# Rotary tables spread by twelve transfers, later rounding of the index sums, slot order, and one moved gate product in a hybrid decoder layer

## The chip, the cores and the metric

The kernel runs on one core of a Trainium2 chip. The metric is the device time of one execution in microseconds (us), as the median of several runs. A profile of one more execution gives the times of single instructions.

## What is computed

One decoder layer on 512 tokens of width 1024, in float32:

```python
proj = x @ w_in
rq, rk, rv, rg, aq, ak, av, iq, ik, iw = jnp.split(proj, IN_SPLITS, axis=-1)
rq, rk, aq, ak, iq, ik = (rope(t, positions) for t in ...)
ret = group_norm(retention_chunkwise(rq, rk, rv)) * gain
ret = jax.nn.silu(rg) * ret
# index: logits[q, h, s] = relu(iq[q, h] . ik[s]); score = sum_h iw[q, h] * logits
sel = indexer_topk(iq, ik, iw, 128)           # 8 index heads of width 64, causal
att = sparse_attention(aq, ak, av, sel)       # softmax over the selected keys
x = layer_norm(ALPHA * x + concat([ret, att]) @ w_out)
gate, up = jnp.split(x @ w_gate_up, 2, axis=-1)
x = layer_norm(ALPHA * x + (silu(gate) * up) @ w_down)
```

## The kernel before

Every large product is made of three matmuls (`mm3`, lines 93 to 96): both operands are split into a rounded part in the format fp32r (names ending in h) and a rest (names ending in l). The split of a weight (`split`, lines 84 to 91) costs a cast on ACT (L86, tile `wh`) and either a subtraction on DVE (L91, tile `wl`) or, for the weights marked Q, a negated copy on ACT (L88) to which a DMA that POOL issues (L89) adds the raw weight.

The order of each engine's instructions is the order in which the program writes them. It has these stages:

1. The index projection (`acc0`, L205), 120 matmuls. Beside it `rotary_tables` works out the angles on DVE and their sines and cosines on ACT. DMAs then copy these from the compact tiles, which hold 256 positions in each half of the partitions, into the tile `tables`: `CT` and `ST` for heads of width 128 (8 transfers on SP's queue, L80), `CI` and `SI` for index heads of width 64 (16 transfers on POOL's queue, L167 and L168).
2. The feature projections (`proj_feature`, tile `pf`): 16 units of 24 matmuls with weights from the ring `wh`/`wl` of 4 buffers. Each unit's result is rotated by `rope` (L217 to L219 on DVE, the sum L221 on POOL) when the next unit has begun.
3. The token projections (`proj_token`, tile `pt`), with retention beside them.
4. The output projection (`mx`) with the attention, then the gate and up products (`g_cycle`, seven products A to D for each of 22 blocks, accumulated in `ga`, `gb`, `gc`), then the down projection.

Beside stages 2 and 3 runs a side chain: `index_rope` (rotation of the index key and queries, their split into h and l parts, and the DMAs that place the halves), `logits` (for each of 8 heads two matmuls on PE, a relu on ACT and one multiply-add on DVE, L375 and L377, on tile `score`), and `topk` (16 pairs of L388 and L389 for each block of 128 queries). `pace` hands out the side chain: in each slot of the main stage it gains a credit and runs the next piece while the credit is positive. `run` calls the side chains of one slot in the order in which they are given.

The psum pool has 4 buffers of the kind `u`, which the logits, the turns of retention (`ret_turn`, tile `rz`, read by `put_mix`, L436 and L437) and the attention scores (`as`, L538) share: a matmul into the fifth buffer waits until the first has been read.

## Time and profile before

| what | value |
|---|---|
| median of 3 runs | 639.75 us (638.44 to 640.84) |
| the profiled execution, its own time | 640.71 us |
| its span from first to last instruction | 638.3 us |
| PE busy | 622.2 us, 97% of the span |
| DVE busy | 486.2 us, 76% |
| ACT busy | 288.4 us, 45% |
| POOL busy | 109.6 us, 17% |
| granted clock of PE, mean | 0.996 |

PE takes the matmuls, PEld loads their weights beside it, DVE, ACT and POOL are the elementwise engines, SP only issues DMAs. Matmuls overlap, so an engine that shows as busy all the time can still have small gaps from one start to the next; times between two starts are given where that matters.

### The profile page before, as it was taken

To read this page: it belongs to the slowest core of one execution; us is meant where nothing else is said; L and a number is where in the kernel's file an instruction comes from. 1 tells how busy PE (TensorE), PEld (TensorE's weight loads), DVE (VectorE), ACT (ScalarE), POOL (GpSimd) and SP (SyncE) were. 2 spreads that over 40 slices of the span, in tenths; PEclk is the share of its full clock that TensorE was granted. 3 is DMA by queue.
4 is the path that set the end of the run, shared out by engine and by line. 5 is a ranking of instruction groups with operands and counts; after the bars stand their busy time and mean duration, and the time that the engine had idled before them with its cause. 6 is when DMAs were issued, how large, how long until landed. Compare 5 with 4: busy or idle time off the path is not lost.

```text
span 638.3 us, 9756 instructions
## 1 busy us (share of the span) xinstructions
PE 622.2 (97%) x3792; PEld 553.8 (87%) x3792; DVE 486.2 (76%) x893; ACT 288.4 (45%) x506; POOL 109.6 (17%) x117
## 2 busy tenths in 40 slices
PE   9999899999999999999999999999999999999995
PEld 7987688888887878888999999999999988888884
DVE  5758886988879877999988989889898874333256
ACT  5603544433343667445655555555455653311100
POOL 1559723321464000141000000000000000000011
PEclk9999999999999999999999999999999999999998
DMA  8865664679544862271823132231323352312002
GB/s 286 295 190 131 157 165 120 160 190 222 133 100 108 315 250 88 74 189 22 227 84 132 67 132 89 110 132 67 132 74 126 132 202 95 132 68 97 1 33 99
DMA packets 23855, 86.66 MB, mean 136 GB/s; under 512 B 2883, under 2 KB 3907, under 8 KB 18179
## 3 DMA queue, kind: packets, MB, share of 16 engines
q1 hardware_dynamic: 18448, 71.32, 32.3%
q0 software_dynamic: 4784, 13.64, 11.0%
q10 hardware_dynamic: 576, 1.11, 0.5%
q8 instruction: 29, 0.48, 0.3%
q14 instruction: 18, 0.12, 0.1%
HBM read 69.80 MB, written 2.10 MB: 113 GB/s over the span
## 4 chain that ended last, share of the span: by engine, by line
PE 54%; DVE 4%; issue 0%; POOLq 0%; ACT 0%; DVEq 0%
PE ga L787 20%; PE gc L787 10%; PE gb L787 5%; PE dl L94 3%; PE dl L96 3%; PE dl L95 3%; PE dr L96 3%; PE dr L94 3%; PE dr L95 3%; DVE wl L91 1%; DVE part L642 0%; PE mx L95 0%; DVE gs L762 0%; PE mx L96 0%; DVE x L615 0%
## 5 line engine op out<-in xcount | busy, mean ns | idle before, releaser
L426 POOL TENSOR_TENSOR rs<-ve,half 128x1 f32<-128x1 f32 (+1 forms) x11 | 13.6, 1238 | 383.7 <-DVE ve L425 383.6
L91 DVE TENSOR_TENSOR dl<-draw,dh 128x1024 fp32r<-128x1024 f32 x22 | 26.9, 1224 | 59.0 <-ACT dh L86 59.0
L86 ACT CAST wh<-raw 128x1024 fp32r<-128x1024 f32 x44 | 46.0, 1049 | 44.6 <-issue 16.7
L86 ACT CAST dh<-draw 128x1024 fp32r<-128x1024 f32 x22 | 23.1, 1052 | 68.0 <-PE dl L96 37.1
L96 PE MATMUL pf<-xh,wl 128*128 128x512 f32 x128 | 50.1, 391 | 2.2 <-DMA wl<-raw 2.2
L94 PE MATMUL pf<-xh,wh 128*128 128x512 f32 x128 | 50.0, 391 | 0.0
L95 PE MATMUL pf<-xl,wh 128*128 128x512 f32 x128 | 49.9, 390 | 0.0
L91 DVE TENSOR_TENSOR wl<-raw,wh 128x1024 fp32r<-128x1024 f32 x25 | 32.4, 1307 | 11.7 <-ACT wh L86 11.7
L94 PE MATMUL pt<-wh,xh 128*128 128x512 f32 x96 | 39.1, 407 | 0.0
L96 PE MATMUL pt<-wh,xl 128*128 128x512 f32 x96 | 37.5, 391 | 0.0
L95 PE MATMUL pt<-wl,xh 128*128 128x512 f32 x96 | 37.4, 390 | 0.0
L94 PE MATMUL dl<-dh,h 128*128 128x512 f32 x88 | 34.2, 389 | 0.0
L95 PE MATMUL dl<-dl,h 128*128 128x512 f32 x88 | 34.2, 389 | 0.0
L96 PE MATMUL dl<-dh,h 128*128 128x512 f32 x88 | 34.2, 389 | 0.0
L95 PE MATMUL dr<-dl,h 128*128 128x512 f32 (+1 forms) x88 | 33.4, 379 | 0.0
L96 PE MATMUL dr<-dh,h 128*128 128x512 f32 (+1 forms) x88 | 33.4, 379 | 0.0
L94 PE MATMUL dr<-dh,h 128*128 128x512 f32 (+1 forms) x88 | 33.4, 379 | 0.0
L96 PEld LDWEIGHTS pf<-xh,wl 128*128 128x128 f32 x128 | 24.0, 188 | 8.1 <-DMA wl<-raw 3.0
L762 DVE TENSOR_TENSOR gs<-graw,gs 128x512 f32<-128x512 f32 x44 | 30.3, 688 | 0.8
L762 DVE TENSOR_TENSOR gs<-graw 128x512 f32<-128x512 f32 x44 | 30.1, 684 | 0.0
L95 PEld LDWEIGHTS pf<-xl,wh 128*128 128x128 f32 x128 | 24.0, 188 | 4.7
L94 PEld LDWEIGHTS pf<-xh,wh 128*128 128x128 f32 x128 | 24.0, 188 | 4.6
(961 smaller groups left out, 1925.3 us busy)
## 6 DMA issues: line engine op xcount, KB each, us to landing
graw<-in_wgu_dram SPq DMA_DIRECT2D x22, 1024.0 KB, 4.8
draw<-in_wd_dram SPq DMA_DIRECT2D x22, 512.0 KB, 4.6
wl<-raw POOLq DMA_DIRECT2D x19, 512.0 KB, 5.8
raw<-in_wf_dram SPq DMA_DIRECT2D x8, 1024.0 KB, 7.5
raw<-in_wo_dram SPq DMA_DIRECT2D x8, 1024.0 KB, 5.7
raw<-in_wt_dram SPq DMA_DIRECT2D x6, 1024.0 KB, 5.0
w0s<-in_w_dram SPq DMA_DIRECT2D x8, 320.0 KB, 5.0
x<-in_x_dram SPq DMA_DIRECT2D x4, 512.0 KB, 5.0
```

The source lines that it names most:

```text
L86: A.copy(hi, src)
L91: eng_lo.tensor_tensor(lo, src, hi.bitcast(F32), op=ALU.subtract)
L94: T.matmul(acc, lhsT=lh, rhs=rh, start=first, stop=False, **kw)
L95: T.matmul(acc, lhsT=lh, rhs=rl, start=False, stop=False, **kw)
L96: T.matmul(acc, lhsT=ll, rhs=rh, start=False, stop=last, **kw)
L426: G.tensor_tensor(r[:, :n], e[:, :n], half[:, :n], op=ALU.pow)
L762: eng.tensor_tensor(t[dst], a, b, op=ALU.subtract)
L787: T.matmul(gp[n][acc], lhsT=a[:, i * S + k * P:i * S + k * P + P], rhs=parts[q][:, b, k], start=first and j == 0, stop=j == 11, skip_group ...
```

## The change

The change has four parts.

- **Tables.** The sines and cosines are written as two tiles `trig`, each with the cosine beside the sine (the second tile with the negated sine), so that one transfer carries both. 8 transfers of 32 partitions fill `CI` and `SI`, 3 of them issued by POOL, 3 by SP and 2 by ACT; 4 transfers of 64 partitions on SP then fill `CT` and `ST`. The cosine is computed twice, and the absolute value comes first on ACT.
- **Index sums.** DVE writes the unrounded sums (`ks`, `qs`); POOL no longer adds them a second time. The rounding (`kh`, `qa`, `qb`) is done by copies on ACT, and all of it stands one step of the side chain later. The first step yields 1.7 instead of 2.7, the last one is followed by one more rounding, and the side chain starts with a credit of 0 instead of -1.
- **Slot order.** Beside `proj_token(0)` the retention and attention chain `tail` now comes ahead of the side chain in each slot.
- **Gate product.** The product D of gate block 1 is taken out of cycle 1 and put into cycle 2, between the two products C, with its weights in a tile of its own (`s9`); the end of block 1 (`g_end`) moves with it.

```diff
--- before.py
+++ after.py
@@ -122,8 +122,9 @@
     CT, ST, CI, SI = (tables[:, i] for i in range(4))
 
     def rotary_tables():
-        both = [tmp("angles"), tmp("turns"), tmp("trig"), tmp("trig_n")]
-        (ang, rr), (hh, kk), (cs, sn), (ng, _) = ((t[:, :H], t[:, H:]) for t in both)
+        both = [tmp("angles"), tmp("turns")]
+        (ang, rr), (hh, kk) = ((t[:, :H], t[:, H:]) for t in both)
+        trig = [tmp(f"trig{q}").rearrange("p (k c) -> p k c", k=2) for q in range(2)]
 
         def sub_mul(dst, mult, const_, src):
             V.scalar_tensor_tensor(dst, in0=mult, scalar=-const_, in1=src, op0=ALU.mult, op1=ALU.add)
@@ -152,20 +153,19 @@
         nearest(kk, ang, 1.0 / TWO_PI)
         sub_mul(ang, kk, TWO_PI, ang)
         yield
-        A.activation(sn, ang, AF.Sin)
         A.activation(rr, ang, AF.Abs)
-        A.activation(cs, rr, AF.Sin, scale=-1.0, bias=cols[:, 2:3])
-        A.activation(ng, ang, AF.Sin, scale=-1.0)
+        for q in range(2):
+            A.activation(trig[q][:, 0], rr, AF.Sin, scale=-1.0, bias=cols[:, 2:3])
+            A.activation(trig[q][:, 1], ang, AF.Sin, scale=(1.0, -1.0)[q])
+        queues = (nc.gpsimd, nc.sync, nc.scalar)
+        for i in range(2):
+            ps, at = slice(64 * i, 64 * i + 64, 2), slice(H * i, H * i + H)
+            for q in range(4):
+                queues[(4 * i + q) % 3].dma_start(tables[32 * q:32 * q + 32, 2:, at], trig[q // 2][ps])
         for i in range(2):
             ps, at = slice(64 * i, 64 * i + 64), slice(H * i, H * i + H)
             for q in range(2):
-                dma(CT[64 * q:64 * q + 64, at], cs[ps])
-                dma(ST[64 * q:64 * q + 64, at], (sn, ng)[q][ps])
-        for i in range(2):
-            ps, at = slice(64 * i, 64 * i + 64, 2), slice(H * i, H * i + H)
-            for q in range(4):
-                nc.gpsimd.dma_start(CI[32 * q:32 * q + 32, at], cs[ps])
-                nc.gpsimd.dma_start(SI[32 * q:32 * q + 32, at], (sn, ng)[q // 2][ps])
+                dma(tables[64 * q:64 * q + 64, :2, at], trig[q][ps])
         yield
 
 
@@ -234,28 +234,37 @@
         G.memset(kk3[:, 1:].bitcast(F32), 0.0)
         A.activation(iwr, acc0[0], AF.Copy, scale=IDX_SCALE)
         t1, t2 = rope(None, acc0[0], CI, SI)
-        V.tensor_tensor(kh, t1, t2, op=ALU.add)
         ks = tmp("ks")
-        G.tensor_tensor(ks, t1, t2, op=ALU.add)
-        for b in (0, 64):
-            s, d = slice(b, b + 32), slice(b + 32, b + 64)
-            G.tensor_tensor(kl[0][s], ks[s], kh[s].bitcast(F32), op=ALU.subtract)
-            nc.gpsimd.dma_start(kl[1][d].bitcast(F32), kl[0][s].bitcast(F32))
-            nc.gpsimd.dma_start(kh[d].bitcast(F32), kh[s].bitcast(F32))
-        yield 2.7
-        for i in range(4):
-            t1, t2 = rope(None, acc0[1 + i], CI, SI, P)
-            V.tensor_tensor(qa[:, i], t1[:, P:], t2[:, P:], op=ALU.add)
-            qs = tmp("qs")
-            G.tensor_tensor(qs[:, P:], t1[:, P:], t2[:, P:], op=ALU.add)
+        V.tensor_tensor(ks, t1, t2, op=ALU.add)
+        yield 1.7
+
+        def halves_k():
+            A.copy(kh, ks)
+            for b in (0, 64):
+                s, d = slice(b, b + 32), slice(b + 32, b + 64)
+                G.tensor_tensor(kl[0][s], ks[s], kh[s].bitcast(F32), op=ALU.subtract)
+                nc.gpsimd.dma_start(kl[1][d].bitcast(F32), kl[0][s].bitcast(F32))
+                nc.gpsimd.dma_start(kh[d].bitcast(F32), kh[s].bitcast(F32))
+
+        def halves_q(i, qs):
+            A.copy(qa[:, i], qs[:, P:])
+            A.copy(qb[:, i], qs[:, P:])
             G.tensor_tensor(ql[:, i], qs[:, P:], qa[:, i].bitcast(F32), op=ALU.subtract)
-            A.copy(qb[:, i], qa[:, i].bitcast(F32))
             if i % 2:
                 n = slice(i - 1, i + 1)
                 for d, s in ((qa[32:64, n], ql[0:32, n]), (qa[96:128, n], ql[64:96, n]),
                              (qb[0:32, n], ql[32:64, n]), (qb[64:96, n], ql[96:128, n])):
                     nc.gpsimd.dma_start(d.bitcast(F32), s.bitcast(F32))
+
+        rounding = halves_k
+        for i in range(4):
+            t1, t2 = rope(None, acc0[1 + i], CI, SI, P)
+            qs = tmp("qs")
+            V.tensor_tensor(qs[:, P:], t1[:, P:], t2[:, P:], op=ALU.add)
+            rounding()
+            rounding = lambda i=i, qs=qs: halves_q(i, qs)
             yield 2.3
+        rounding()
         yield 3.0
         iwp = psu("iwp")
         for j in range(1, NB):
@@ -579,7 +588,7 @@
     lg = chain(*[logits(j) for j in range(1, NB)])
     tk = chain(*[topk(j) for j in range(1, NB)])
     side = chain(index_rope(), lg, tk)
-    run(chain(*[proj_feature(c) for c in range(4)]), pace(side, 0.85, -1.0))
+    run(chain(*[proj_feature(c) for c in range(4)]), pace(side, 0.85))
     run(chain(*[proj_feature(c) for c in range(4, 8)]), pace(side, 0.85))
     run(proj_token(1), pace(side, 1.7))
     rt["decay"] = big.tile([P, 2, HEADS * P], F32, tag="s7", name="decay")
@@ -588,7 +597,7 @@
     rets = retention()
     run(proj_token(2), pace(side, 1.8), pace(rets, 1.2))
     tail = chain(rets, att_score(0))
-    run(proj_token(0), pace(side, 0.9), pace(tail, 1.4))
+    run(proj_token(0), pace(tail, 1.4), pace(side, 0.9))
     drain(tail)
 
 
@@ -761,13 +770,19 @@
         for dst, a, b in ((0, u[:, :S], g[:, :S]), (1, u[:, S:], t[0]), (2, u[:, S:], u[:, :S]), (3, g[:, S:], t[1]))[which]:
             eng.tensor_tensor(t[dst], a, b, op=ALU.subtract)
 
+    def held(n):
+        return n == FIRST - 3
+
     def g_conv(n, kind, eng=V, into=None):
         if n >= NF:
             return
         g, u, t = graw[n][:, 0], graw[n][:, 1], gsum.get(n)
         src = {"A": lambda: (t[1], t[0]), "B": lambda: (g[:, :S], g[:, S:]), "C": lambda: (t[2], t[3]),
                "D": lambda: (u[:, S:],)}[kind]()
-        if into:
+        if kind == "D" and held(n):
+            both = big.tile([P, 2, S], F32R, tag="s9", name="dheld")
+            h, l = both[:, 0], both[:, 1]
+        elif into:
             hl = big.tile([P, 2, 1024], F32R, tag=into, name=f"g{n}{kind}")
             h, l = hl[:, 0], hl[:, 1]
         else:
@@ -815,7 +830,7 @@
     def g_cycle(n, between=None):
         nxt = n + 1 if FIRST <= n + 1 < NF else None
         g_mm(n, "a", "A", 0, "s2", False)
-        if n:
+        if n and not held(n - 1):
             g_end(n - 1)
         if between:
             next(between)
@@ -835,6 +850,8 @@
         if nxt:
             g_t1(nxt)
             g_mm(nxt, "b", "B", 1, "12", True)
+        if held(n - 1):
+            g_mm(n - 1, "c", "D", 0, "s4", False)
         c = gp[n]["c"]
         if n == NF - 1:
             c = tmp("gc")[:, :Q]
@@ -844,6 +861,8 @@
         V.tensor_tensor(gp[n]["t7"], gp[n]["t7"], c, op=ALU.add)
         if between:
             next(between)
+        if held(n - 1):
+            g_end(n - 1)
         if n == 0:
             g_conv(1, "A")
         if n + 2 >= FIRST:
@@ -857,7 +876,7 @@
         if n == 0:
             for m in range(FIRST):
                 g_silu1(m)
-        if n < NF - 1:
+        if n < NF - 1 and not held(n):
             g_mm(n, "c", "D", 0, "s4", False)
         A.activation(gp[n]["h2"], gp[n]["a"], AF.Silu)
         g_conv(n + 1, "D", V if n else None)
```

On ACT, at the end of stage 1, before (`trig` and `trig_n` are the compact sines and cosines, `wh_372` and `wh_376` the first two feature weights):

```order
L86 CAST w0h_307<-w0s_83 128x640
L155 ACT_TABLE_LOAD
L155 ACTIVATE trig<-angles 128x256
L156 ACTIVATE angles<-angles 128x256
L157 ACTIVATE trig<-angles,cols 128x256
L158 ACTIVATE trig_n<-angles 128x256
L86 CAST wh_372<-raw_275 128x1024
L86 CAST wh_376<-raw_275 128x1024
```

and after the change:

```order
L86 CAST w0h_307<-w0s_83 128x640
L156 ACTIVATE angles<-angles 128x256
L158 ACT_TABLE_LOAD
L158 ACTIVATE trig_175<-angles,cols 128x256
L159 ACTIVATE trig_175<-angles 128x256
L158 ACTIVATE trig_176<-angles,cols 128x256
L159 ACTIVATE trig_176<-angles 128x256
L164 DMA tables<-trig_176 32x2x256
L164 DMA tables<-trig_175 32x2x256
L86 CAST wh_361<-raw_275 128x1024
L86 CAST wh_365<-raw_275 128x1024
```

The load of the sine table now stands behind the absolute value, and a fifth activation and two DMA issues stand ahead of the first feature weight.

On POOL, in the index part of stage 2, before (`ks`, `qs` are the second sums, `wl_483` the second weight that POOL finishes):

```order
L239 TENSOR_TENSOR ks<-rt_415,rt_416 128x512
L242 TENSOR_TENSOR kk_359<-ks,kk_359 32x512
L243 DMA kk_359<-kk_359 32x512
L244 DMA kk_359<-kk_359 32x512
L242 TENSOR_TENSOR kk_359<-ks,kk_359 32x512
L243 DMA kk_359<-kk_359 32x512
L244 DMA kk_359<-kk_359 32x512
L221 TENSOR_TENSOR akT<-rt_445,rt_446 128x512
L250 TENSOR_TENSOR qs<-rt_466,rt_467 128x384
L251 TENSOR_TENSOR ql<-qs,qa 128x384
L89 DMA wl_483<-raw_279 128x1024
```

and after the change:

```order
L245 TENSOR_TENSOR kk_348<-ks,kk_348 32x512
L246 DMA kk_348<-kk_348 32x512
L247 DMA kk_348<-kk_348 32x512
L245 TENSOR_TENSOR kk_348<-ks,kk_348 32x512
L246 DMA kk_348<-kk_348 32x512
L247 DMA kk_348<-kk_348 32x512
L221 TENSOR_TENSOR akT<-rt_441,rt_442 128x512
L252 TENSOR_TENSOR ql<-qs,qa 128x384
L89 DMA wl_479<-raw_279 128x1024
```

Two additions, `ks` and the first `qs`, are gone ahead of the weight's DMA; three more `qs` are gone behind it, and the rest stands in the same order.

On DVE, near the end of stage 3 (`mrl` is the rest of a turned retention block, L388/L389 and L397/L398 a pair of `topk`), right behind the first of the four turned blocks, before:

```order
L91 TENSOR_TENSOR wl_1792<-raw_1449,wh_1791 128x1024
L388 MAX m_1801<-score 128x8
L389 MATCH_REPLACE score<-m_1801,score 128x512
L502 TENSOR_SCALAR rz<-ri_1746,mv,rs 128x128 x4
L437 TENSOR_TENSOR mrl<-rz_1821,mrh 128x4x128
L388 MAX m_1836<-score 128x8
L389 MATCH_REPLACE score<-m_1836,score 128x512
L437 TENSOR_TENSOR mrl<-rz_1839,mrh 128x4x128
L91 TENSOR_TENSOR wl_1847<-raw_1449,wh_1846 128x1024
L388 MAX m_1868<-score 128x8
L389 MATCH_REPLACE score<-m_1868,score 128x512
L437 TENSOR_TENSOR mrl<-rz_1871,mrh 128x4x128
```

and after the change:

```order
L91 TENSOR_TENSOR wl_1787<-raw_1444,wh_1786 128x1024
L511 TENSOR_SCALAR rz<-ri_1738,mv,rs 128x128 x4
L397 MAX m_1801<-score 128x8
L398 MATCH_REPLACE score<-m_1801,score 128x512
L446 TENSOR_TENSOR mrl<-rz_1816,mrh 128x4x128
L446 TENSOR_TENSOR mrl<-rz_1831,mrh 128x4x128
L397 MAX m_1838<-score 128x8
L398 MATCH_REPLACE score<-m_1838,score 128x512
L91 TENSOR_TENSOR wl_1842<-raw_1444,wh_1841 128x1024
L446 TENSOR_TENSOR mrl<-rz_1863,mrh 128x4x128
```

Between the first and the last of the four `mrl` stand two pairs of `topk` instead of three.

## Rows read from the trace of the kernel before

**Rows 1.** The page of the kernel before: part 1, busy us by engine.
```profile
PE 622.2 (97%) x3792; PEld 553.8 (87%) x3792; DVE 486.2 (76%) x893; ACT 288.4 (45%) x506; POOL 109.6 (17%) x117
```

**Rows 2.** Waits of PE: operation, releaser: total us, times, longest us.
```profile
PE pf L96 <- DMA wl<-raw: 2.2, 2, 1.4
PE as L538 <- DVE mrl L437: 1.4, 1, 1.4
PE lg L369 <- DVE score L375: 1.4, 1, 1.4
...
PE ga L787 <- ACT gt L843: 0.9, 2, 0.5
```

**Rows 3.** Timeline of PE: start us, us, instruction, [idle before <-releaser].
```profile
28.45 0.39 PE L96 MATMUL pf<-xh,wl 128*128 128x512 f32 x1
...
56.61 0.50 PE L96 MATMUL pf<-xh,wl 128*128 128x512 f32 x1 [0.78 <-DMA wl<-raw]
...
77.51 0.39 PE L96 MATMUL pf<-xh,wl 128*128 128x512 f32 x1
79.29 0.39 PE L369 MATMUL lg<-kk,qa 128*128 128x256 f32 x1 [1.39 <-DVE score L375]
...
83.02 0.39 PE L369 MATMUL lg<-kk,qb 128*128 128x256 f32 x1 [0.32 <-DVE score L377]
...
318.99 0.39 PE L787 MATMUL ga<-part,gh2C 128*128 128x256 f32 x1 [0.46 <-ACT gt L843]
```

**Rows 4.** Timeline of DVE, 24 to 79 us.
```profile
24.39 3.49 DVE L91 TENSOR_TENSOR wl<-raw,wh 128x1024 fp32r<-128x1024 f32 x3
38.35 0.69 DVE L217 TENSOR_TENSOR rt<-acc,tables 128x512 f32<-128x512 f32 x1 [10.47 <-DMA tables<-trig]
...
41.13 2.31 DVE L91 TENSOR_TENSOR wl<-raw,wh 128x1024 fp32r<-128x1024 f32 x1
...
78.75 0.48 DVE L375 TENSOR_SCALAR score<-lg,iw 128x256 f32<-128x256 f32 x1
```

**Rows 5.** Instructions on the tile tables: duration ns min/median/max; landing of its DMAs.
```profile
L80 SPq DMA_DIRECT2D tables<-trig x6: 498/599/606, 23.1 to 26.9; - x6
...
DMA to landing us min/median/max: 2.8/3.7/7.8
```

**Rows 6.** Timeline of POOL, 23 to 32 us: first and last table transfer.
```profile
23.41 0.74 POOL L167 DMA_DIRECT2D tables<-trig  x1 [16.59 <-ACT trig_n L158]
...
31.33 0.51 POOL L168 DMA_DIRECT2D tables<-trig_n  x1
```

**Rows 7.** Timeline of ACT, 18 to 48 us.
```profile
18.79 1.28 ACT L155 ACT_TABLE_LOAD   x1
21.83 0.42 ACT L155 ACTIVATE trig<-angles 128x256 f32<-128x256 f32 x1 [1.76 <-DVE angles L129]
...
23.32 3.11 ACT L86 CAST wh<-raw 128x1024 fp32r<-128x1024 f32 x3
...
47.84 0.51 ACT L252 CAST qb<-qa 128x384 fp32r<-128x384 f32 x1 [13.35 <-DVE qa L248]
```

**Rows 8.** Windows: us, busy (x) of PE, PEld, DVE, ACT, POOL; clock, DMA share, GB/s.
```profile
24.00:31.00 7.00, 7.00 (x36) 6.24 (x36) 3.88 (x4) 4.84 (x6) 6.90 (x15) 1.00 0.68 167
```

**Rows 9.** Windows of the tile pf alone: us, busy (x) of PE, PEld, DVE; clock, DMA share, GB/s.
```profile
28.00:55.00 27.00, 27.00 (x120) 22.32 (x120) 4.12 (x6) 1.00 0.57 153
```

**Rows 10.** Timeline of POOL, 49 to 52 us: the second weight that POOL finishes.
```profile
49.94 1.00 POOL L250 TENSOR_TENSOR qs<-rt,rt 128x384 f32<-128x384 f32 x1
...
51.99 0.91 POOL L89 DMA_DIRECT2D wl<-raw  x1
```

**Rows 11.** Timeline of DVE, 205 to 207 us.
```profile
205.42 0.69 DVE L388 MAX8 m<-score 128x8 f32<-128x512 f32 x1
...
206.81 0.68 DVE L437 TENSOR_TENSOR mrl<-rz,mrh 128x512 fp32r<-128x512 f32 x1
```

**Rows 12.** The chain that ended last: start us, us, piece.
```profile
320.69 1.44 PE gc L787 x12
```

## Prediction

> **What bounds the kernel now.** I read the page first, then the waits of PE, then PE's own timeline at each wait, and last the engine that each wait names. PE is busy for 622.2 of 638.3 us [rows 1], and its matmuls run in the order of the program. So the time is PE's work plus the gaps in which PE waits, and only what removes or adds such a gap counts; DVE, ACT and POOL may gain as much as they like elsewhere. The waits of PE [rows 2] name the gaps that this change can reach: two in the feature projections, where a weight's rest `wl` lands late (2.2 us together), two in the first logits, where the scores on DVE have not freed a psum buffer (1.39 and 0.32 us [rows 3]), one before the attention scores, behind the last `mrl` (1.4 us), and two behind the copy L843 (0.9 us together).
>
> The idle time that a row gives is a little short of the loss. From the start of the last feature matmul at 77.51 to that of the logits matmul at 79.29 are 1.78 us [rows 3], while 120 feature matmuls in a row take 27.00 us, 0.225 us from start to start [rows 9]. That is 1.55 us lost where the row says 1.39, and the first matmul after a wait takes some 0.1 us longer to hand over. I count 0.25 us on top of each wait. The feature gaps are then 2.2 + 0.5 = 2.7 us, the logits gaps 1.71 + 0.5 = 2.2 us, the score gap 1.4 + 0.25, and the gate gap that is touched 0.46 + 0.25 = 0.7 us.
>
> Where do the first two kinds come from? DVE has its three first weight rests done by 24.39 + 3.49 = 27.88 us and then stands idle for 10.47 us until the tables have landed, at 38.35 [rows 4]. From there to the first score at 78.75 it has no time left: 40.4 us of work behind which PE, ACT and POOL wait. ACT sits idle for 13.35 us behind DVE's first index sum before it can go on to the next weights, at 47.84 [rows 7]; POOL then adds `qs` (1.00 us) before it issues that weight's DMA at 51.99 [rows 10]. PE waits for this weight. It is one late start that is paid three times.
>
> **Part 1, the tables.** POOL issues 16 transfers, the first at 23.41, the last at 31.33 [rows 6]; a table transfer lands in 2.8 to 7.8 us, 3.7 in the median [rows 5], and the last took about the 7 us until 38.35. Now POOL issues 3, SP 3 and then 4, ACT 2. The price lies on ACT. Before, the sine table was loaded (1.28 us at 18.79) while ACT waited for the angles; the first sine ran at 21.83, and the first weight cast at 23.32, so an activation costs 1.49 / 4 = 0.37 us [rows 7]. After, five activations (1.87), the load (1.28, now after the angles) and two issues (at most 0.6 each, as SP's [rows 5]) stand between 21.83 and the first cast: 21.83 + 4.35 = 26.2, which is 2.9 us later. Its cast takes 3.11 / 3 = 1.04 [rows 7], the rest on DVE 3.49 / 3 = 1.16 [rows 4]: ready at 28.4. PE takes this rest with its third feature matmul, which started at 28.45 [rows 3]. So it just fits; I take 0.2 us of wait, between 0 and 1.2; the upper end is two issues of twice the length.
>
> The row of the load has 1.28 us and the engine was idle behind it, so the trace cannot show what a load costs when work is queued. The Trainium skill, "ScalarE: Activation LUTs", section "What ACT_TABLE_LOAD costs", puts a drain of about 1.38 us beside those 1.28, 2.66 us in all; by it the wait of PE here would be an estimated 1.6 us instead of 0.2.
>
> The index transfers are all issued by about 26.2, so they land at 29.9 by the median and at 34.0 by the slowest of today. DVE's three weight rests, 2.9 us later than before, end at 30.8. DVE therefore starts the rotation at 30.8 instead of 38.35, 7.5 us earlier; at the slow bound it is 34.0 and 4.3 us.
>
> **Part 2, the index sums.** The four `qa` copies and `kh` are added on ACT, each about 0.51 us [rows 7], where ACT waited 13.35 us for DVE; this cover stays, since the copies wait for the same sums. If it went, the weight casts queued behind them would be 2.5 us later, still inside the margin below. POOL loses five additions. They also slow DVE while they run: a weight rest beside them took 2.31 instead of 1.16 us [rows 4]. I count no gain for that and keep it as reserve.
>
> Feature gaps: ACT's cast and POOL's DMA both follow DVE, and POOL has two additions fewer ahead of this DMA. Before, it was issued at 51.99 and PE went on with it at 56.61 [rows 3, 10], 4.6 us later. Now it is issued at 51.99 - 7.5 = 44.5 at the latest and landed at 49.1. PE asks for it with the third matmul of the sixth unit, at 28.45 + 120 x 0.225 = 55.45. The second gap has the same chain. Both go, 2.7 us, and at the slow bound they still go.
>
> Logits: the first logits matmul now stands behind 162 feature matmuls instead of 186, so PE asks 24 x 0.225 = 5.4 us earlier. The fifth head, the first that needs a freed buffer, stands behind 177 of them (before: 201): 28.0 + 177 x 0.225 + some 1.3 us of logits and turns = 69.1 us. DVE has one weight rest (1.2) and one rotation (2.1) less ahead of the first score, 40.4 - 3.3 = 37.1 us of work: 30.8 + 37.1 = 67.9 us. It fits with 1.2 us to spare, and the 2.2 us go. At the slow bound the score comes at 71.1, and 2.0 us of the gap stay.
>
> **Part 3, slot order.** The last `mrl` ran at 206.81, behind a `topk` pair that began at 205.42: 1.39 us a pair [rows 11]. With one pair fewer ahead of it, it ends 1.4 us earlier; DVE is busy without a break there, so all of it reaches PE. 1.4 of the 1.65 us go. The pairs come later beside weight rests that PE needs only in the output projection, several us on; they cost nothing there.
>
> **Part 4, the gate product.** The 12 matmuls of a product take 1.44 us [rows 12]. Put into the wait of 0.7 us before 318.99 [rows 3] they cover it whole. The same product leaves the end of cycle 1, so cycle 2 starts 1.44 us sooner; the weights of its first product are cast a cycle ahead, and a rest that came late would cost tenths of a us. Gain 0.7 us. The like wait one cycle before is not touched. `g_end` of block 1 comes later on DVE, and nobody waits for it in that cycle.
>
> **Sum.** -2.7 - 2.2 - 1.4 - 0.7 + 0.2 = -6.8 us from 640.7, the profiled execution's own time: 633.9. The median of the runs shown lies 1.0 us lower, which would give 632.9. I predict 633.4 us.
>
> **Rivals.**
>
> - *The tables land late because the transfers themselves are the limit.* Both kernels move 1 MB in rows of 1 KB, and between 24 and 31 us, with table transfers nearly alone, the DMA engines were 68% busy at 167 GB/s [rows 8]. At that rate 1 MB takes 6.3 us; if three queues are served in turn, the index half is done with the rest, at 24.3 + 6.3 + 2.8 = 33.4 us. The first score is then 1.4 us late, with some of the second logits gap: 635.5 us. For it speaks the busy share, against it that SP sends the index transfers ahead of the others and that the issue alone took 7.9 us. The Trainium skill, "DMA: Bandwidth & Descriptors", section "Rules for kernel authors", says that spreading transfers over SP, ACT and GpSimd does not help bandwidth and only saves issue time; it speaks for this rival as far as bandwidth is the limit. Chance 0.15.
> - *The load of the sine table holds ACT longer than its row.* The 1.76 us of idle time behind the load [rows 7] would then not have been a wait for the angles alone, and with those the first cast ends late: PE waits up to 1.9 us near 28, which gives 635.2 us. For it speaks only that the row cannot exclude it; against it, that the angles are named as the releaser. The page on ScalarE cited above, of the Trainium skill, would bear this rival out. Chance 0.07.
> - *Slower: the logits were pulled forward further than the tables.* If ACT's or SP's transfers land behind the next 1 MB weight, or DVE is held, so that the rotation starts at T, PE waits T + 37.1 - 69.1 us in the logits. From T of about 37.5 on the change loses: at today's 38.35 that is 6.3 us instead of 2.2, the feature gaps stay, and with parts 3 and 4 the time is 640.7 + 4.1 - 2.1 + 0.2 = 642.9; above 643 from there on. The 3 us between 34 and 37 speak against it. Chance 0.06.
> - *The waits move.* Copies on ACT and the heads that now come in other groups cost a new wait of 2 to 4 us in stage 2, and only half of the gain is left: 637.3 us. Chance 0.13.
>
> **Numbers.** The forecast has 0.59, with 631.0 to 635.0 as its own range; the lower end is all gaps whole from the median of 639.75. With the first, second and fourth rival the range of 631.0 to 638.2 holds about 8 in 10, allowing for some of the fourth lying above and for sizes I have not seen. A measurement of this kernel tells about 0.5%, 3.2 us, from no change. Faster by more than that, under 636.5, are the forecast and nearly all of the first two rivals: 0.78. Slower 0.06, within 0.16.
>
> **What would show it.** In the profile after: the wait of DVE for the tables ending near 31 us; no wait of `pf` for a DMA of `wl`; no wait of `lg` for a score before 85 us; the wait of `as` under 0.5 us; one wait of `ga` behind the copy of `gt` instead of two; a first `pf` wait of at most 0.4 us near 28 us. I am wrong if DVE starts its rotation after 34 us, or if waits of PE with other names add up to more than 2 us before 210 us.

## The result and the profile after

| | before | changed |
|---|---|---|
| median of 4 runs each, us | 639.94 (638.44 to 640.84) | 634.21 (633.38 to 634.84) |
| ratio, 95% interval | | 0.9912 (0.9889 to 0.9935) |
| the profiled execution, us | 640.71 | 633.38 |
| its span, us | 638.3 | 631.6 |

The changed kernel is faster by 5.7 us in the medians; 633.4 us had been predicted, in a range of 631.0 to 638.2. Part 1 of its page, busy us by engine [rows 1]:

```profile
PE 620.1 (98%) x3792; PEld 553.9 (88%) x3792; DVE 483.3 (77%) x893; ACT 291.9 (46%) x512; POOL 94.7 (15%) x99
```

The waits of PE in the changed kernel (operation, releaser: total us, times, longest us) stand against [rows 2]:

```profile
PE as L547 <- DVE mrl L446: 1.3, 1, 1.3
...
PE ga L802 <- ACT gt L860: 0.5, 1, 0.5
PE ga L802 <- DVE parts L651: 0.3, 1, 0.3
```

Both waits of `pf` for a weight's DMA and both of `lg` for a score are gone, of the two of `ga` behind `gt` one is left, and the wait of `as` is still there: 1.31 us where it had 1.43. From start to start, the measure of the prediction, the four kinds lost 2.75 (`pf`), 2.59 (`lg`), 1.79 (`as`) and 1.44 us (`ga` behind `gt`) before and lose 0, 0, 1.66 and 0.72 now. That is 6.2 of the 6.7 us by which the span is shorter. Most of the rest lies in stage 1: the first feature matmul starts at 27.64 instead of 27.98 us, and among the profiles of this study it starts anywhere from 27.5 to 28.5.

The chain that removed them begins on ACT. Its timeline behind the last cast of stage 1 (start us, us, instruction, idle before and releaser), against [rows 7]:

```profile
20.73 0.42 ACT L156 ACTIVATE angles<-angles 128x256 f32<-128x256 f32 x1 [3.37 <-DVE angles L130]
21.17 1.28 ACT L158 ACT_TABLE_LOAD   x1
22.46 0.51 ACT L158 ACTIVATE trig<-angles,cols 128x256 f32<-128x256 f32 x1
...
24.02 1.63 ACTq L164 DMA_DIRECT2D tables<-trig  x2
25.74 2.00 ACT L86 CAST wh<-raw 128x1024 fp32r<-128x1024 f32 x2 [1.76 <-PE acc L205]
```

The instructions on `tables` (count: duration ns min/median/max, first and last start) and the landing of its transfers, against [rows 5, 6]:

```profile
L80 SPq DMA_DIRECT2D tables<-trig x4: 605/618/861, 25.5 to 27.7; - x4
L164 SPq DMA_DIRECT2D tables<-trig x3: 600/647/732, 23.3 to 24.8; - x3
L164 POOL DMA_DIRECT2D tables<-trig x3: 557/583/752, 23.6 to 24.9; - x3
L164 ACTq DMA_DIRECT2D tables<-trig x2: 741/796/850, 24.0 to 24.8; - x2
...
DMA to landing us min/median/max: 2.2/2.8/3.8
```

And DVE at the places of [rows 4], the first weight rests, the first rotation and the first score:

```profile
26.83 3.50 DVE L91 TENSOR_TENSOR wl<-raw,wh 128x1024 fp32r<-128x1024 f32 x3 [3.45 <-ACT wh L86]
31.12 0.69 DVE L217 TENSOR_TENSOR rt<-acc,tables 128x512 f32<-128x512 f32 x1 [0.79 <-ACT iwr L235]
...
65.71 0.48 DVE L384 TENSOR_SCALAR score<-lg,iw 128x256 f32<-128x256 f32 x1 [2.62 <-ACT lg L380]
```

The index transfers are issued by 25.7 and take 3.8 us at most. DVE starts the rotation at 31.12 instead of 38.35, and the row no longer names a DMA: it waits 0.79 us for ACT's copy `iwr`. At 65.71 DVE stands idle until a relu is done, so it has caught up with PE; the fifth head runs at 69.27 without a wait.

### The profile page after: what moved, and what is told of

It is laid out like the page before. It is cut to its first block, busy times and chain, and to the rows that moved or that the text cites. A ratio compares the mean times of both kernels' runs of the same rounds, so it can differ in the third digit from the quotient of the medians.

```text
span 631.6 us, 9734 instructions
## 1 busy us (share of the span) xinstructions
PE 620.1 (98%) x3792; PEld 553.9 (88%) x3792; DVE 483.3 (77%) x893; ACT 291.9 (46%) x512; POOL 94.7 (15%) x99
## 4 chain that ended last, share of the span: by engine, by line
PE 54%; DVE 4%; issue 0%; POOLq 0%; ACT 0%; DVEq 0%
PE ga L802 20%; PE gc L802 10%; PE gb L802 5%; PE dl L96 3%; PE dl L95 3%; PE dl L94 3%; PE dr L96 3%; PE dr L95 3%; PE dr L94 3%; DVE wl L91 1%; DVE part L651 0%; PE mx L95 0%; DVE gs L771 0%; PE mx L96 0%; DVE x L624 0%
## 5 line engine op out<-in xcount | busy, mean ns | idle before, releaser
L86 ACT CAST dh<-draw 128x1024 fp32r<-128x1024 f32 x22 | 23.2, 1053 | 68.0 <-PE dl L96 37.1
L91 DVE TENSOR_TENSOR wl<-raw,wh 128x1024 fp32r<-128x1024 f32 x25 | 30.6, 1235 | 17.2 <-ACT wh L86 17.2
L96 PE MATMUL pt<-wh,xl 128*128 128x512 f32 x96 | 37.5, 391 | 0.0
L95 PE MATMUL dr<-dl,h 128*128 128x512 f32 (+1 forms) x88 | 33.4, 379 | 0.0
L96 PE MATMUL dr<-dh,h 128*128 128x512 f32 (+1 forms) x88 | 33.4, 379 | 0.0
L94 PE MATMUL dr<-dh,h 128*128 128x512 f32 (+1 forms) x88 | 33.4, 379 | 0.0
```

The source lines that it names most:

```text
L86: A.copy(hi, src)
L91: eng_lo.tensor_tensor(lo, src, hi.bitcast(F32), op=ALU.subtract)
L94: T.matmul(acc, lhsT=lh, rhs=rh, start=first, stop=False, **kw)
L95: T.matmul(acc, lhsT=lh, rhs=rl, start=False, stop=False, **kw)
L96: T.matmul(acc, lhsT=ll, rhs=rh, start=False, stop=last, **kw)
```

## The experiments

Each kernel was timed in several rounds beside the kernel before. "Less" is its median against that of before in the same series, since these lay between 639.9 and 640.8; the ratio is the one on record for the rounds and need not be the quotient of the two medians. The idle times are those of PE's rows. Only the intervals of pool_adds and same_step lie clear of that of the change; among the others it is the rows of the waits that tell the kernels apart, not the times.

| kernel | median us | before us | less | ratio (95% interval) | pf | lg | as | others |
|---|---|---|---|---|---|---|---|---|
| the change | 634.21 | 639.94 | 5.7 | 0.9912 (0.9889, 0.9935) | 0 | 0 | 1.3 | ga 0.5 |
| tables_only | 635.19 | 640.22 | 5.0 | 0.9922 (0.9905, 0.9939) | 0 | 0 | 1.3 | ga 0.9 |
| tables_back | 636.14 | 640.22 | 4.1 | 0.9942 (0.9923, 0.9960) | 0 | 1.3 | 1.3 | ga 0.5 |
| slots_back | 635.25 | 640.22 | 5.0 | 0.9926 (0.9910, 0.9942) | 0 | 0 | 1.6 | rz 1.0, ga 0.5 |
| gate_back | 634.73 | 640.22 | 5.5 | 0.9916 (0.9899, 0.9932) | 0 | 0 | 1.3 | ga 0.9 |
| pool_adds | 639.10 | 640.77 | 1.7 | 0.9975 (0.9964, 0.9986) | 0.3 | 3.0 | 1.3 | ga 0.5 |
| same_step | 639.93 | 640.77 | 0.8 | 0.9991 (0.9981, 1.0001) | 3.9 | 0 | 1.5 | ga 0.5 |
| one_queue | 634.41 | 640.77 | 6.4 | 0.9910 (0.9896, 0.9925) | 0 | 0 | 1.5 | ga 0.5 |
| hold_two | 634.95 | 640.77 | 5.8 | 0.9914 (0.9901, 0.9927) | 0 | 0 | 1.5 | ga on gl1A 0.5 |
| no_sums | 634.39 | 640.78 | 6.4 | 0.9898 (0.9879, 0.9916) | 0 | 0 | 1.5 | ga 0.5 |
| pace06 | 633.87 | 640.78 | 6.9 | 0.9893 (0.9874, 0.9911) | 0 | 0 | 0 | ga 0.5 |
| no_sums06 | 633.74 | 640.78 | 7.0 | 0.9893 (0.9874, 0.9912) | 0.5 | 0 | 0 | apt 1.1, ga 0.5 |
| decay_early | 633.02 | 640.32 | 7.3 | 0.9880 (0.9857, 0.9904) | 0 | 0 | 0 | ga 0.5 |

### The tables alone, and everything but the tables

**tables_only** is the kernel before with the new `rotary_tables` (the first two hunks of the diff) and nothing else.

> The kernel before with only the tables of the change (12 transfers on three queues, absolute value first). Theory: the late start of DVE is the cause of all the waits of pf and lg, so this part alone removes them: rotation from about 31 us, no wait of pf for a DMA of wl, no wait of lg for a score, 640.0 - 5.3 = 634.7 us; the waits of as (1.4) and of both ga behind gt (0.9) stay. Rival: POOL's additions of the sums are needed for it too (a weight's DMA still issued behind them), and the feature waits stay in part: 636 to 637.5 us.

Measured: 5.0 us less, no wait of `pf` or `lg`, and the waits that other parts were to take stand where they stood:

```profile
PE as L538 <- DVE mrl L437: 1.3, 1, 1.3
...
PE ga L787 <- ACT gt L843: 0.9, 2, 0.5
```

The theory holds: the early start alone removes both kinds of wait, with POOL's second additions and the immediate rounding still in place.

**tables_back** is the changed kernel with the old `rotary_tables`.

```diff
...
-        queues = (nc.gpsimd, nc.sync, nc.scalar)
...
+                nc.gpsimd.dma_start(CI[32 * q:32 * q + 32, at], cs[ps])
+                nc.gpsimd.dma_start(SI[32 * q:32 * q + 32, at], (sn, ng)[q // 2][ps])
```

> The changed kernel with only the tables as before: 16 index transfers issued by POOL and 8 by SP, separate sines and cosines, sine first on ACT; index sums, slot order and gate product stay changed. Theory of the prediction (rival 'slower'): the rotation on DVE starts near 38 us instead of 31.1, the first logits wait some 6 us and the feature projections 2.7 us, so 634.2 + 6.3 + 2.7 = 643 us, slower than the kernel before. Rival: the profile of the changed kernel shows DVE idle for 5.4 us between 31 and 66 us and the first score 3.1 us ahead of the fifth head at 69.27; these 8.5 us take up a start that is 7.2 us later, so the logits wait at most 1 us and the time is 634.2 to 637.9, below the kernel before.

Measured: 4.1 us less than before, not 2 or 3 us more. The rotation starts at 37.58, 0.8 us earlier than in the kernel before, and still no feature matmul waits. The only new wait of `lg` is for a transfer of `qa`, not for DVE:

```profile
PE lg L378 <- DMA qa<-ql: 1.3, 1, 1.3
```

Why, show the instructions of DVE from the first rotation to just ahead of the first score (line, operation, count | busy us, mean ns | idle before and releaser). Before, 38.3 to 78.7 us:

```profile
L91 DVE TENSOR_TENSOR wl<-raw,wh 128x1024 fp32r<-128x1024 f32 x4 | 7.1, 1765 | 3.1 <-ACT wh L86 3.1
L248 DVE TENSOR_TENSOR qa<-rt,rt 128x384 fp32r<-128x384 f32 x4 | 6.2, 1552 | 0.1
...
L217 DVE TENSOR_TENSOR rt<-pf,tables 128x512 f32<-128x512 f32 x7 | 4.8, 682 | 0.0
```

tables_back, 37.5 to 67.3 us:

```profile
L263 DVE TENSOR_TENSOR qs<-rt,rt 128x384 f32<-128x384 f32 x4 | 4.2, 1052 | 0.2
...
L217 DVE TENSOR_TENSOR rt<-pf,tables 128x512 f32<-128x512 f32 x6 | 4.1, 681 | 0.0
L91 DVE TENSOR_TENSOR wl<-raw,wh 128x1024 fp32r<-128x1024 f32 x3 | 3.7, 1218 | 0.0
```

The stretch shrank from 40.4 us to 29.8 (37.58 to 67.37). A rest took 1.77 us in the mean and takes 1.22, an index sum 1.55 and now 1.05: together 2.2 + 2.0 = 4.2 us. The 3.1 us in which DVE waited for ACT's casts are gone too, and a rotation and a rest fewer stand ahead of the first score (3.3 us). So the two big parts of the change each remove nearly all of the waits of `pf` and `lg`, one by starting DVE earlier, the other by giving it less to do and, as the next runs show, by what it takes out of POOL's queue. Their gains don't add.

What lengthens the rests and the sums is POOL. A rotation's multiply, which reads `pf` from psum and `tables` from SBUF, took 682 and 681 ns in the two kernels; a rest or a sum, with both operands in SBUF, took up to 2.31 and 2.62 us in these stretches beside POOL's tensor operations, 1.22 and 0.56 without. Each one that took longer began while a tensor operation of POOL was running. The longest sum of before, and the addition of POOL beside it:

```profile
65.95 2.62 DVE L248 TENSOR_TENSOR qa<-rt,rt 128x384 fp32r<-128x384 f32 x1
```

```profile
66.83 1.32 POOL L250 TENSOR_TENSOR qs<-rt,rt 128x384 f32<-128x384 f32 x1
```

The addition ends at 68.15, the sum at 68.57. The Trainium skill, "SBUF — State Buffer", section "SBUF: two separate sides", says that a GpSimd operation that reads SBUF and a DVE operation with two SBUF inputs share one pair of ports as an exclusive lock, and that the one that comes second waits for the whole other instruction; these rows agree. In the stretch of before the rests and sums took 6.2 us more than their own time, and beside each of the four longest one of POOL's second additions (`ks` or `qs`) was running; in tables_back 2.0 us are left.

### Which half of the index sums part does it

Both runs start from tables_back, where the early tables don't hide the difference.

**same_step** puts the rounding back right behind its addition; **pool_adds** leaves it a step later and has POOL add the query sums again.

```diff
+        halves_k()
+        yield 1.7
...
-            rounding()
-            rounding = lambda i=i, qs=qs: halves_q(i, qs)
+            halves_q(i, qs)
...
```

```diff
...
             rounding()
-            rounding = lambda i=i, qs=qs: halves_q(i, qs)
+            qg = tmp("qg")
+            G.tensor_tensor(qg[:, P:], t1[:, P:], t2[:, P:], op=ALU.add)
+            rounding = lambda i=i, qs=qs, qg=qg: halves_q(i, qs, qg)
```

> The run with the tables as before (636.1 us) with the other thing put back: the rounding of each sum stands right behind its addition, not a step later; POOL has no second additions. Theory P (POOL's additions are what cost): no change, 635.7 to 636.6 us, no wait of pf for a weight's DMA. Theory D (the step's delay is the cure): ACT's weight casts and POOL's weight DMA are queued behind unmade sums again, the feature projections wait 1 to 2.7 us: 637 to 639 us.

> The run with the tables as before (636.1 us: late start, changed index sums) with one thing put back: POOL adds the four query sums a second time and works on its own sum, the rounding still one step later on ACT. Theory P: the index sums part helps because POOL's additions no longer slow DVE (a rest took 2.31 us beside them instead of 1.22, a sum up to 2.62 instead of 0.56). Then DVE's sums and rests grow again, its work from the start of the rotation to the first score goes from 29.6 to 32 us or more, the logits wait grows by 2 to 3 us: 638 to 639.5 us. Theory D: it helps because the rounding comes a step later and no weight cast on ACT or weight DMA on POOL is queued behind a sum that DVE has not made; then 636.1 to 636.6 us.

Measured: the gain against before falls from 4.1 us to 0.8 with the immediate rounding and to 1.7 with the additions. (Part of both losses is TensorE's clock, as the last section shows. And since the gate product, 0.72 us by PE's rows, is still in these kernels, almost nothing is left in same_step of what the index sums gave.) In same_step POOL's queue shows the cause (timeline, with idle time and releaser): `ql` waits for ACT's rounding of a sum that DVE has just made, four placing transfers follow it, and only then comes the weight's DMA, at 55.06; in tables_back it was issued at 48.81, right behind the first `ql` (second block).

```profile
51.77 1.02 POOL L254 TENSOR_TENSOR ql<-qs,qa 128x384 fp32r<-128x384 f32 x1 [1.57 <-ACT qa L252]
53.08 1.00 POOL L259 DMA_DIRECT2D qa<-ql  x2 [0.30 <-POOL ql L254]
54.08 0.99 POOL L259 DMA_DIRECT2D qb<-ql  x2
55.06 0.96 POOL L89 DMA_DIRECT2D wl<-raw  x1
```

```profile
47.86 1.00 POOL L252 TENSOR_TENSOR ql<-qs,qa 128x384 fp32r<-128x384 f32 x1
48.81 0.92 POOL L89 DMA_DIRECT2D wl<-raw  x1
```

PE wants that weight at 55.7 and gets it at 59.77. So the delay is needed, as theory D said, and it cost more than the 1 to 2.7 us that it gave.

In pool_adds theory P has the size but not the way. DVE's stretch grew by 0.7 us only, from 29.8 to 30.5 (37.70 to 68.19). What grew is the wait of `lg` for `qa`: POOL's queue is longer by its additions, the transfers that place the halves are issued 0.8 us later (66.45 instead of 65.63), and they land more slowly, for a reason that these runs do not show (DMA issues from 60 to 74 us: count, KB, median us to landing; tables_back, then pool_adds).

```profile
qa<-ql POOLq DMA_DIRECT2D x2, 96.0 KB, 4.6
```

```profile
qa<-ql POOLq DMA_DIRECT2D x2, 96.0 KB, 5.9
```

Both halves of the part matter, then, and both through what stands in POOL's queue. Neither alone brings back the time for which DVE was held up: beyond their own time the rests and sums ahead of the first score took 2.6 us in pool_adds and 1.2 in same_step, against 6.2 before.

### One queue instead of three

```diff
-        queues = (nc.gpsimd, nc.sync, nc.scalar)
+        queues = (nc.sync, nc.sync, nc.sync)
```

> The changed kernel with all 12 table transfers issued by SP instead of three queues. Theory: what counts is that 8 transfers carry the index half instead of 16; at 0.65 us each SP has issued them 5.2 us behind 23.3, at 28.5, landed near 31; DVE was held until 31.1 by ACT's copy iwr anyway and has some 8 us to spare, so 634.2 us. Rival (spreading over queues is what counts): rotation starts at 33 us or later, and the next weight's transfer, issued behind the tables at 30.0, comes 2.5 us later; then PE waits in the feature projections and the time is 635 to 637 us.

Measured: 6.4 us less than before, 0.9910, where the change has 0.9912. The rotation starts 0.55 us later and does wait for a transfer, which costs nothing:

```profile
31.67 0.69 DVE L217 TENSOR_TENSOR rt<-acc,tables 128x512 f32<-128x512 f32 x1 [2.47 <-DMA tables<-trig]
```

The three queues bring nothing that can be measured. What is left for the early start is that 8 transfers instead of 16 carry the index half, that SP sends them ahead of the others, and that POOL, whose 16 issues took 7.9 us before, has none; which of these counts, no run here separates. The Trainium skill, "DMA: Bandwidth & Descriptors", section "Rules for kernel authors", says that spreading over issuing engines saves only issue time; the trace agrees, and the issue time saved here lay beside DVE's rests.

### The gate product

```diff
-        return n == FIRST - 3
+        return False
```

for **gate_back**, and `return n in (0, 1)` for **hold_two**, with `s8` as the second block's tile.

> The changed kernel without the moved gate product (block 1's product D back at the end of cycle 1). Theory: the wait of ga for the copy of gt in cycle 2 comes back, 0.46 us idle and 0.7 from start to start, 634.9 us. Rival: with the rest of the kernel earlier that copy is no longer late, no change, 634.2 us.

> The changed kernel with the product D of block 0 also moved one cycle on, into the wait for the copy of gt that is left in cycle 1 (0.52 us idle, 0.72 from start to start). Theory: as for block 1, the 1.44 us of product cover the wait: 633.5 us. Rival: the product leaves the end of cycle 0, where it covered the cast of block 1's first weights on ACT and DVE; PE waits there instead, 0.5 to 1.5 us: 634.0 to 635.0 us.

Measured: in gate_back the wait is back with 0.46 us, 0.72 from start to start, at 313.59; the medians differ by 0.5 us, which the intervals don't tell from nothing. In hold_two the wait in cycle 1 goes too, and a new one stands at the head of the cycle, 0.77 us from start to start, as the rival said:

```profile
PE ga L802 <- DVE gl1A L91: 0.5, 1, 0.5
```

The product of block 0 had covered the rest of block 1's first weights. One product can be moved for a gain, the next one can't.

### The wait of the attention scores

**slots_back** undoes only the slot order: `pace(side, 0.9), pace(tail, 1.4)`.

> The changed kernel with the slot order of before beside proj_token(0) (side chain ahead of the tail). Prediction's step: one pair of topk more ahead of the last mrl, the wait of as grows by 1.4 us to 2.7, 635.6 us. Rival: the wait of as was 1.43 before and is 1.31 in the changed kernel, so the pair that left was made up for by one more pair ahead of POOL's rstate; if that second pair comes from the earlier side chain and not from the slot order, restoring the order costs 1.4 us; if it comes from the slot order itself, it costs 0.2 us at most, 634.2 us.

Measured: 0.8 us less gain than the change had (the intervals overlap), with the wait of `as` at 1.6 and a new one of 1.0 us for POOL's `rzz`. So the order is worth something in the changed kernel, though tables_only has the old order and the wait of `as` there is 1.3. The next run takes back the index sums part, the one that brings the side chain forward (`pace(side, 0.85, -1.0)` and the old `index_rope`; **no_sums**); **pace06** leaves a pair of `topk` for later, `pace(side, 0.6)`; **no_sums06** does both.

> The changed kernel with the index sums part taken back (sums, rounding, yields and credit as before); tables, slot order and gate product stay changed. Theory: the wait of as fell by only 0.13 us in the changed kernel because its earlier side chain puts a fifth pair of topk ahead of POOL's rstate (4 before); the slot order by itself takes a pair out behind it. With the sums part back, both counts are the lower ones (4 and 5), the wait of as falls from 1.31 to 0.4 us at most, and since the tables alone already removed the waits of pf and lg the time is 634.3 - 1.2 = 633.1 us, faster than the changed kernel. Rival: the wait of as does not follow these pairs; it stays at 1.3 us and the time is 634.3 to 634.8 us.

> The changed kernel with the side chain's credit beside proj_token(0) at 0.6 instead of 0.9 a slot: one pair of topk fewer between rstate and the last mrl (4 instead of 5), two pairs more beside the output projection. Theory: the last mrl comes 1.4 us earlier, the wait of as goes to 0.1 us, 632.9 us. Rival: the pairs left over delay the attention scores of the blocks 1 to 3 or a weight rest in the output projection by as much: 634.3 us or more.

> Both of the other two: the index sums part taken back and 0.6 instead of 0.9 credit a slot (4 pairs ahead of ve, 4 between rstate and the last mrl). Theory: the wait of as has nothing left to give after either one, so 632.9 to 633.2 us, as the better of the two. Rival: four pairs more beside the output projection make the scores or weight rests there late, 633.5 us or more.

Measured: pace06 did what was expected, no wait of `as` is left; against `as` the last `mrl` comes 1.2 us earlier, of which 0.4 is not the pair's but an earlier start of DVE's retention work (below). no_sums06 has none either, but the pairs it leaves over make a softmax late (`apt` behind DVE's `ast`, 1.1 us), so its rival holds in part. no_sums gave 634.4 as its rival had said, with a wait of 1.5. Its DVE rows show why, at the first product with the table `decay` and the last `mrl`:

```profile
153.49 0.69 DVE L456 TENSOR_TENSOR rst<-rs,decay 128x512 f32<-128x512 f32 x1 [3.86 <-DMA decay<-in_decay_dram]
...
201.82 0.68 DVE L437 TENSOR_TENSOR mrl<-rz,mrh 128x512 fp32r<-128x512 f32 x1
```

In the kernel before (its last `mrl` is in [rows 11]) and in the changed one, with DVE's waits for POOL's `rstate` between:

```profile
157.44 0.69 DVE L456 TENSOR_TENSOR rst<-rs,decay 128x512 f32<-128x512 f32 x1 [2.50 <-DMA decay<-in_decay_dram]
...
171.70 0.69 DVE L475 TENSOR_TENSOR rstate<-rstate,rkv 128x512 f32<-128x512 f32 x1 [2.18 <-POOL rstate L474]
...
186.52 0.69 DVE L475 TENSOR_TENSOR rstate<-rstate,rkv 128x512 f32<-128x512 f32 x1 [3.31 <-POOL rstate L474]
```

```profile
152.10 0.69 DVE L465 TENSOR_TENSOR rst<-rs,decay 128x512 f32<-128x512 f32 x1 [2.21 <-DMA decay<-in_decay_dram]
...
165.58 0.69 DVE L484 TENSOR_TENSOR rstate<-rstate,rkv 128x512 f32<-128x512 f32 x1 [2.17 <-POOL rstate L483]
...
181.90 0.69 DVE L484 TENSOR_TENSOR rstate<-rstate,rkv 128x512 f32<-128x512 f32 x1 [3.30 <-POOL rstate L483]
...
201.11 0.68 DVE L446 TENSOR_TENSOR mrl<-rz,mrh 128x512 fp32r<-128x512 f32 x1
```

From this product to the last `mrl` DVE needs 49.37 us before (157.44 to 206.81), 49.01 in the changed kernel and 48.33 in no_sums. So the slot order does take out about a pair, 1.0 us here, and the earlier side chain of the index sums part gives 0.7 of it back. The two waits for `rstate`, as long in every kernel, show where. Behind the second one the new order leaves 5 pairs of `topk` instead of 6: 19.21 us to the last `mrl` for 20.29. Between the two, the earlier side chain puts 6 pairs instead of 5, 16.32 us for 14.82; ahead of the first, 6 instead of 7, 13.48 us for 14.26.

But the start of the stretch is set by `decay`, whose transfer SP issues behind the weights of stage 3 and which lands 7.9 us after its issue before, 8.1 in the changed kernel and 9.8 in no_sums and in slots_back. In these four kernels, in tables_only and in pace06, stage 3 takes from its first matmul to its last the time to this product, plus the stretch, plus 6.3 us. So the loss of slots_back is not the order's alone: against the changed kernel its stretch is 0.86 us longer (49.87), and it starts 0.98 us later in the stage (29.25 for 28.27).

**decay_early** is no_sums with that load some 70 us earlier, and with `mixt[0]`, whose rest takes the same tile `s10`, allocated at the first turn:

```diff
+        if b == 0:
+            mixt[0] = unit("s8", "mrh", F32R), unit("s10", "mrl", F32R)
...
+    rt["decay"] = big.tile([P, 2, HEADS * P], F32, tag="s10", name="decay")
+    dma(rt["decay"], decay_d)
     run(chain(*[proj_feature(c) for c in range(4, 8)]), pace(side, 0.85))
     run(proj_token(1), pace(side, 1.7))
-    rt["decay"] = big.tile([P, 2, HEADS * P], F32, tag="s7", name="decay")
-    dma(rt["decay"], decay_d)
-    mixt[0] = unit("s8", "mrh", F32R), unit("s10", "mrl", F32R)
```

> The run without the changed index sums (tables, slot order and gate product changed; 634.4 us, wait of as 1.5) with one thing more: the table decay is loaded some 45 us earlier, into a tile of its own. In that run DVE stood idle for 3.86 us until decay had landed, 9.8 us after its issue, and its retention work began 1.1 us later against PE than in the kernel before (2.50 us of wait, landed in 7.9). Theory: this late landing hid what one pair of topk fewer ahead of the last mrl is worth; with decay in time DVE starts on PE's turn instead, at least 1.1 us earlier, the wait of as falls from 1.5 to 0.4 us or less, 633.2 us. Rival: DVE catches up at POOL's rstate in any case, and the wait of as stays at 1.3 to 1.5 us, 634.4 us.

(The load was put further ahead than the 45 us that the expectation names, at 72.7 instead of 143.6.) Measured: 633.02 us, the fastest of the study, 7.3 us less than before. Its DVE rows and PE's longest waits:

```profile
149.84 0.68 DVE L456 TENSOR_TENSOR rst<-rs,decay 128x512 f32<-128x512 f32 x1
...
199.70 0.69 DVE L437 TENSOR_TENSOR mrl<-rz,mrh 128x512 fp32r<-128x512 f32 x1 [0.20 <-ACT mrh L436]
```

```profile
PE warm L188 <- DVE cold L185: 1.2, 1, 1.2
PE ga L794 <- ACT gt L852: 0.5, 1, 0.5
```

No wait of `as` is left. The interval of its ratio overlaps that of the change, so the 1.6 us between the two gains is not proven by the times alone; the row of the wait is.

## Why the prediction was right, and where it was not

- **The total.** -5.7 us in the medians where the working had -6.8; the 633.4 us predicted, between two bases, lie 0.8 us below the median measured. Three of the four gains came as forecast; one did not.
- **Start, +0.2: measured 0.1.** The first cast ran at 25.74 for a forecast of 26.2, and that it was not later is luck. From the first activation to the cast ACT took 5.01 us for a forecast of 4.35, mainly because its two issues took 1.63 us for at most 1.2. The load took no more than its row: `Abs` ends at 21.15 and the first sine starts at 22.46, 1.31 us later, with its input waiting. The 1.38 us beside it that the Trainium skill names ("ScalarE: Activation LUTs", "What ACT_TABLE_LOAD costs") do not show here, and that rival is out. The angles also came 1.1 us earlier than in the profile of before, of which the sum knew nothing; in tables_back they came 0.85 us earlier too, so most of it belongs to the execution. In the profiles of the other kernels with this order on ACT the wait is 0 to 0.4 us.
- **Rotation at 30.8: measured 31.12**, with the bandwidth rival's 33.4 out. The releaser is ACT's `iwr`, which the working left out; the tables would have allowed an earlier start.
- **Feature waits, -2.7: measured -2.75. Logits, -2.2: measured -2.59.** The fifth head runs at 69.27 for a forecast of 69.1, the first score at 65.71 for 67.9. The size was right; the reason "one late start that is paid three times" was only half of it. The late start is enough to cause these waits (tables_only), but not all that does: with the start as late as ever, the index sums part removes them too (tables_back).
- **The slower rival** failed in its price. The step that DVE "has no time left: 40.4 us of work", cut to 37.1, is wrong: 3.1 us of it were waits for ACT, and 4.2 us were rests and sums held up beside POOL, which the prediction had seen and kept "as reserve". With 29.8 us instead of 37.1 a start at 37.6 is still in time.
- **Slot order, -1.4: measured -0.13.** The step that failed is "DVE is busy without a break there, so all of it reaches PE". DVE's work up to the last `mrl` is a chain from the landing of `decay` on, with two waits for POOL in it. The pair that left was worth 1.0 us in no_sums, not 1.39; the earlier side chain of part 2 took 0.7 of that back, and the chain began 0.25 us later in stage 3 than before (28.27 us behind its first matmul for 28.02). The rows shown of before began at 205 us, too late to see that. So the sign "the wait of `as` under 0.5 us" did not come.
- **Gate product, -0.7: measured -0.72**, and in gate_back the wait returns with the same size.
- The rivals "the tables land late" and "the waits move" did not come: no wait of PE stands between 29 and 201 us.

## What to carry to other kernels

When two edits aim at one wait, undo each alone before adding their gains: here the tables were worth 5.0 us, the rest without them 4.1, and all together 5.7. A stretch in which an engine seems to have no time left is not its work; look in it for short waits and for instructions that take longer than others of the same form. And where a chain on a saturated engine ends late, follow it back to where the engine last stood idle for something from outside the chain: what ended that idle time (here the load of a small table behind large ones) may be cheaper to move than anything behind it.

## What was not expected of the hardware

A wait of PE can cost more than its own length. In same_step PE stood idle for 3.92 us; the matmuls behind it start 0.42 us apart instead of 0.23 for some 3 us, with the granted clock at 0.50, which is 1.2 instead of 2.4 GHz. PE's timeline, and its windows (us, busy of PE, PEld, DVE, ACT, POOL; clock, DMA share, GB/s):

```profile
59.77 0.50 PE L96 MATMUL pf<-xh,wl 128*128 128x512 f32 x1 [3.92 <-DMA wl<-raw]
...
60.60 0.63 PE L96 MATMUL pf<-xh,wl 128*128 128x512 f32 x1
61.02 0.63 PE L94 MATMUL pf<-xh,wh 128*128 128x512 f32 x1
...
64.22 0.39 PE L96 MATMUL pf<-xh,wl 128*128 128x512 f32 x1
```

```profile
60.80:63.40 2.60, 2.60 (x7) 2.03 (x7) 2.51 (x5) 0.00 (x0) 1.28 (x1) 0.50 1.01 328
64.00:66.00 2.00, 2.00 (x12) 1.65 (x11) 1.66 (x3) 2.00 (x4) 1.40 (x2) 1.00 0.00 0
```

The seven matmuls from 60.60 to 63.58 take 2.98 us where seven at the full rate take 1.6, so 1.4 us are lost on top of the wait. pool_adds shows the same behind its wait of 2.98 us (granted clock 0.50 from 74 to 76 us); behind the waits of before, 1.4 us at most in this stretch, the windows show 1.00. It explains most of what the waits leave open: the spans of these two lie 4.4 and 3.3 us above that of tables_back, and the waits of `pf` and `lg`, which from start to start lose 4.1 us in same_step, 3.6 in pool_adds and 1.7 in tables_back, account for 2.4 and 1.9 of that. The clock does not fall in every execution: three of the 12 of pool_adds have a mean granted clock of 0.997 and spans of 635.1 to 635.3 us, the other nine 0.992 to 0.995 and 636.5 to 638.5. What sets them apart, the one profile of this kernel cannot show.
